# Even mixer of an encoder trunk: rotary partner added by transfers, load phase by arrival, residual kept in DRAM

## The chip, the cores and the metric

The kernel runs on one core of a Trainium2 chip. The metric is the device time of one execution in microseconds (us), lower is better. The core has TensorE (PE, with its weight loads PEld), VectorE (DVE), ScalarE (ACT), GpSimd (POOL) and SyncE (SP), which here only issues transfers. Each engine works through its own instructions in order and waits at semaphores for the others.

## What is computed

The reference is an encoder trunk of two layers with 512 positions of 1024 channels in float32. Cut to what matters:

```
for i in 0, 1:
    h += 0.5 * SwiGLU_1(RMSNorm(h))            # 1024 -> 2 x 2816 -> 1024
    if i == 0:   h += W_out [A | B]            # the even mixer
    else:        h += W_out NA2D(RMSNorm(h))   # the odd mixer
    h += 0.5 * SwiGLU_2(RMSNorm(h))
    h += sigmoid(RMSNorm(h) @ W_gate) * (p[i] @ W_ple)
out = RMSNorm(h)

A: 12 query heads and 4 key/value heads of 64, window |i-j| <= 128,
   a sink logit per head, rotary positions on q and k
B: 4 slots, each with three dilated windows (128,1), (512,4), (2048,16),
   rotary, the three outputs merged by their softmax denominators
```

The rotary step takes a projection p of two heads (128 channels x 512 positions) to p*cos + partner(p)*sin, where the partner of a channel lies 32 channels away in the same head.

## The kernel before

Activations lie with channels on the 128 partitions and the 512 positions along the row, eight chunks of 128 channels for h. Every float32 product is made of three matmuls on parts: a value is split into a high part, rounded to the matmul's type, and a low part, the rest; `mm3` (L154) multiplies high by high, high by low and low by high. Weights come in units of 128x1024 (512 KB) by SP's queue into `wr`; `split` (L132) makes the high part on ScalarE (L133, a copy) and the low part by a subtraction (L134) on VectorE, or in the mixers for every third unit on GpSimd (`lo_eng`, L136). The pool of activations has 62 tiles of 128x512, the small pool `tmp` ten. PSUM has three banks `mm`, two `sc`, two `tr` and one `ob`.

**The load phase.** `setup` (L96) runs idle matmuls first (WARM, L112). It loads the eight chunks of h, the gate unit after chunk 0 and the up unit after chunk 5 (UP_AT), and writes the splits of the chunks (`norm_split`, L183 on ScalarE and L184 on VectorE) and of the units as code in chunk order; a scheduler sets the final order by priorities. `pair_front` (L235) then multiplies all of the gate unit and all of the up unit, 24 matmuls each.

**Feed-forwards.** Four pairs go through `pair_front`, a pair at 4 through `pair`, and the pairs from 5 on through `pair_fast` (L298), which multiplies with fewer products on sums of halves. One of its sums of weights is made by an accumulating transfer on GpSimd's queue (L308), and its half unit `rb` is a tile of the small pool (L304). The residual is stored to DRAM when a feed-forward begins and loaded again in its down projection (L369 to L391). In the even mixer h stays in SBUF.

**The even mixer.** `ab` (L584) builds two lists. The steps are softmax and value steps: `a_steps` (L679) with scores and softmax of a head (`a_soft`, L706; scores at L575, mask, scaling and maximum at L576) and the product with the values (transposes at L496, products at L507), and `b_steps` (L722) with scores, softmax and a merge over the three windows (L758 on; its scalings at L785, its transposes at L794). The fill is TensorE work that needs no softmax: 20 projections of 24 matmuls, four value projections of 96 shorter ones and parts of the output projection. `weave` (L650) puts fill between the steps by weights and by what each step needs; then `out_proj` (L530) does the rest and adds h.

The norm's factor R comes from sums of squares by `stat` (L199): matmuls, a scaling on VectorE (L206), a power on GpSimd (L207), a transposition on TensorE (L223). `rope` (L541) multiplies R into the tables of cosines and sines once. Then, for every projection, VectorE shuffles lanes within groups of 32 (L551) and multiplies by the cosines (L552), GpSimd multiplies the shuffled copy by the sines (L553), and VectorE adds both (L556, L559, L562, by the order in which positions are written). For this, weights lie in memory with the channels of a head permuted, so that a partner is 16 lanes away. `stack_q` (L409) puts the high and low part of a query, 64 lanes each, above each other (L416 on ScalarE, L417 on VectorE). `stack_k` (L421) does the like for keys with a copy by SP's queue (L429), a subtraction on GpSimd (L430) into tiles whose other half is zeroed (L439). The finished mixture is split with its low part on GpSimd (`split_chunk`, L674).

## Time and profile before

| | us |
|---|---|
| median of three runs | 2096.43 |
| the three runs | 2096.35, 2096.43, 2098.21 |
| the profiled execution | 2097.75 |
| its span on the core | 2095.8 |

The profiled execution's time includes 1.95 us outside the span. Its granted TensorE clock has a mean of 0.993. The page has busy times by engine; rows of the view by windows give the same for one stretch, with the number of instructions in brackets. A row of the waits names the engine and line that waited, the engine, tile and line that ended the wait, and the us in total, the times and the longest. A row of the timeline has start and duration, in brackets the idle time before it and what ended that. Rows by groups have the count, then busy us and mean ns, then idle time before; rows by line have the least, median and greatest duration in ns. Line numbers in rows of before are those of the code above.

| stretch, us of the span | stage |
|---|---|
| 0 to 26 | load phase and first pair |
| 26 to 367 | rest of the first feed-forward |
| 367 to 652 | even mixer, with its output projection |
| 652 to 1030 | second feed-forward |
| 1030 to 2096 | gated embedding, layer 1, last norm |

### The profile page before, as it was taken

The page shows a single profiled execution, that of the slowest core. Times are in us where ns is not written, and L with a number is a line of the kernel's source. Part 1 is how long each engine was busy: PE and PEld are TensorE (multiplying, and loading weights), DVE is VectorE, ACT ScalarE, POOL GpSimd, SP SyncE. Part 2 cuts the span into 40 slices and gives each one's busy share as a digit, 9 for nine tenths or more (in the row PEclk, how much of TensorE's full clock was granted, in tenths as well). Part 3 has the DMA queues.
Part 4 walks back from the last instruction along what each step waited for, and adds up shares of the span by engine and source line. Part 5 has one row for each costly group of instructions (what it writes and reads, how often), then busy time and mean ns, then how long its engine had stood idle before and what let it go on. Part 6 is the DMA issues. An engine that isn't in the chain of part 4 may idle for free.

```text
span 2095.8 us, 31959 instructions
## 1 busy us (share of the span) xinstructions
PE 2047.1 (98%) x12400; PEld 1813.2 (87%) x12400; DVE 1403.4 (67%) x2449; ACT 978.1 (47%) x1661; POOL 284.1 (14%) x221
## 2 busy tenths in 40 slices
PE   9999999999999999999999999999999999999998
PEld 6999988777787899988888999888888789998886
DVE  7878733699786887752459877434778787775334
ACT  5455522565544455442345555323656545554232
POOL 0000011233211000001110000013222200000111
PEclk9999999999999999999999999999999999999999
DMA  6666533221223466643334665433333346665331
GB/s 181 164 178 173 161 119 109 92 70 56 66 68 130 111 170 165 169 151 114 118 129 122 176 167 158 146 119 121 106 106 97 120 110 169 171 169 151 108 113 41
DMA packets 103063, 270.59 MB, mean 129 GB/s; under 512 B 19968, under 2 KB 27648, under 8 KB 102912
## 3 DMA queue, kind: packets, MB, share of 16 engines
q1 hardware_dynamic: 92976, 232.87, 34.2%
q0 software_dynamic: 9792, 35.66, 10.2%
q8 instruction: 97, 1.59, 0.3%
q14 instruction: 54, 0.44, 0.1%
q10 hardware_dynamic: 144, 0.04, 0.0%
HBM read 253.83 MB, written 8.88 MB: 125 GB/s over the span
## 4 chain that ended last, share of the span: by engine, by line
PE 82%; DVE 7%; ACT 4%; DMA 4%; issue 2%; POOL 1%; SPq 0%; ACTq 0%; DVEq 0%; POOLq 0%
PE mm L158 9%; PE mm L159 9%; PE mm L157 9%; PE sc L157 6%; PE sc L159 6%; PE sc L158 6%; PE mm L330 5%; PE mm L331 5%; PE mm L332 5%; DMA tmp<-in_gu_dram 3%; PE sc L332 2%; PE sc L331 2%; PE sc L330 2%; DVE wl L134 2%; ACT wh L133 2%
## 5 line engine op out<-in xcount | busy, mean ns | idle before, releaser
L133 ACT ACTIVATE wh<-wr 128x1024 fp32r<-128x1024 f32 (+2 forms) x430 | 439.2, 1035 | 669.3 <-PE mm L158 180.8
L134 DVE TENSOR_TENSOR wl<-wr,wh 128x1024 fp32r<-128x1024 f32 (+2 forms) x413 | 501.0, 1217 | 319.7 <-ACT wh L133 317.8
L157 PE MATMUL mm<-act,wh 128*128 128x512 f32 (+1 forms) x1016 | 399.0, 393 | 2.8 <-ACT act L183 2.4
L158 PE MATMUL mm<-act,wh 128*128 128x512 f32 (+1 forms) x1016 | 400.0, 394 | 1.4 <-POOL act L134 0.6
L159 PE MATMUL mm<-act,wl 128*128 128x512 f32 (+1 forms) x1016 | 398.1, 392 | 0.0
L330 PE MATMUL mm<-act,wh 128*128 128x256 f32 x1088 | 312.9, 288 | 7.6 <-ACT tmp L348 4.2
L332 PE MATMUL mm<-act,wl 128*128 128x256 f32 x1088 | 308.2, 283 | 0.0
L331 PE MATMUL mm<-act,wh 128*128 128x256 f32 x1088 | 308.2, 283 | 0.0
L159 PE MATMUL sc<-act,wl 128*128 128x512 f32 (+1 forms) x594 | 231.4, 389 | 0.6 <-DVE wl L134 0.6
L157 PE MATMUL sc<-act,wh 128*128 128x512 f32 (+1 forms) x594 | 231.9, 390 | 0.0
L158 PE MATMUL sc<-act,wh 128*128 128x512 f32 (+1 forms) x594 | 231.4, 390 | 0.0
L157 PEld LDWEIGHTS mm<-act,wh 128*128 128x128 f32 x1016 | 191.8, 189 | 41.2 <-ACT act L183 3.6
L158 PEld LDWEIGHTS mm<-act,wh 128*128 128x128 f32 x1016 | 192.1, 189 | 40.5 <-DVE act L184 2.4
L159 PEld LDWEIGHTS mm<-act,wl 128*128 128x128 f32 x1016 | 192.1, 189 | 36.4
L330 PEld LDWEIGHTS mm<-act,wh 128*128 128x128 f32 x1088 | 208.5, 192 | 14.3 <-ACT tmp L348 8.4
L331 PEld LDWEIGHTS mm<-act,wh 128*128 128x128 f32 x1088 | 208.7, 192 | 0.3
L332 PEld LDWEIGHTS mm<-act,wl 128*128 128x128 f32 x1088 | 208.7, 192 | 0.2
L197 POOL TENSOR_TENSOR ssq<-ssq,tmp 128x512 f32<-128x512 f32 x48 | 78.4, 1634 | 684.6 <-ACT tmp L190 684.5
L332 PE MATMUL sc<-act,wl 128*128 128x256 f32 x544 | 155.1, 285 | 1.5 <-DVE wl L134 1.5
L330 PE MATMUL sc<-act,wh 128*128 128x256 f32 x544 | 154.7, 284 | 1.0 <-ACT wh L133 0.8
L331 PE MATMUL sc<-act,wh 128*128 128x256 f32 x544 | 154.1, 283 | 0.0
L308 POOL DMA_DIRECT2D wr<-in_gu_dram x68 | 59.2, 871 | 699.4 <-DMA wr<-in_gu_dram 244.9
(180 smaller groups left out, 3541.9 us busy)
## 6 DMA issues: line engine op xcount, KB each, us to landing
wr<-in_gu_dram SPq DMA_DIRECT2D x176, 512.0 KB, 4.1
wr<-in_gu_dram POOLq DMA_DIRECT2D x68, 512.0 KB, 5.4
wr<-in_dn_dram SPq DMA_DIRECT2D x64, 512.0 KB, 3.8
tmp<-in_gu_dram SPq DMA_DIRECT2D x68, 256.0 KB, 4.6
wr<-in_dn_dram SPq DMA_DIRECT2D x32, 384.0 KB, 3.2
wr<-in_qk_ab_dram SPq DMA_DIRECT2D x20, 512.0 KB, 3.2
wr<-in_plg_dram SPq DMA_DIRECT2D x16, 512.0 KB, 3.2
wr<-in_qk_c_dram SPq DMA_DIRECT2D x16, 512.0 KB, 3.3
```

Of the source, the lines that this page charges most:

```text
L133: self.nc.scalar.activation(hi, src, AF.Copy)
L134: (lo_eng or self.nc.vector).tensor_tensor(lo, src, hi.bitcast(F32), op=ALU.subtract)
L157: mm(out, stat[0], mov[0], start=start, stop=False)
L158: mm(out, stat[0], mov[1], start=False, stop=False)
L159: mm(out, stat[1], mov[0], start=False, stop=stop)
L197: eng.tensor_tensor(self.acc, self.acc, sq, op=ALU.add)
L308: nc.gpsimd.dma_start(rs, w[:, :UNIT], accum_op=ALU.add)
L330: mm(out, w[0][:, c], xs[k][0][:, x], start=start and k == 0, stop=False, skip_group_check=True)
L331: mm(out, w[0][:, c], xs[k][1][:, x], start=False, stop=False, skip_group_check=True)
L332: mm(out, w[1][:, c], xs[k][0][:, x], start=False, stop=stop and k == half - 1, skip_group_check=True)
```

## The change

It has six parts.

1. **Load phase.** WARM goes from 14 to 12 and UP_AT from 5 to 3. The splits of chunks and units are written six chunks behind the loads (LEAD), in the order in which the data are to arrive, with the gate unit in three pieces, and the scheduler keeps that order. The first pair's up products start at k = 3 between the gate products. The next pair's units come behind the last split.
2. **Rotary partner by transfers.** The lanes are no longer permuted. VectorE multiplies the projection by the sines into `u` and by the cosines into `o` (after L595, L596), already in the order wanted; four accumulating transfers of 32x512 (64 KB) on GpSimd's queue then add `u` to `o`, each 32 lanes to the 32 beside them (after L599). The mixer has 20 such steps, so 80 transfers.
3. **Stacks a chunk later.** `stacked` parts the projection and rotary step from the stack, and `behind_next` puts each stack behind the next fill item.
4. **No arithmetic on GpSimd in the even mixer**, but for the power and the zeroing: low parts of weights, of keys and of the mixture go to VectorE, and the two wide scalings of each A softmax (L719) to ScalarE. The mixture's split comes a step later (`split_later`).
5. **Start and weave.** The first two projections go to the two `sc` banks ahead of the norm's factor; six fill items come ahead of the first softmax step; A steps weigh 1.3 for 1; two B steps claim what they need two steps earlier (BEGIN_B).
6. **Tiles.** The even mixer stores h to DRAM and loads it in its output projection (`put_away`, `fetch`). The small pool has eight tiles instead of ten, and `rb` two of its own.

The diff, cut to this:

```diff
-WARM = 14
+WARM = 12
-UP_AT = 5
+UP_AT = 3
+LEAD = 6
-TMPS = 10
+TMPS = 8
+BEGIN_B = 26, 32
...
+        pieces = {0: ((0, 0, q), (0, q, 2 * q)), 1: ((0, 2 * q, UNIT),), UP_AT: ((1, 2 * q, UNIT), (1, 0, 2 * q))}
+        self.pinned = True
+        for n in range(KC + LEAD):
...
+            c = n - LEAD
+            if c >= 0:
+                last = self.norm_split(c)
+                for j, a, b in pieces.get(c, ()):
+                    self.split(*(y[:, a:b] for y in units[j]))
...
-        return self.nc.vector if self.turn else self.nc.gpsimd
+        return self.nc.vector if self.turn or self.alone else self.nc.gpsimd
...
+                for k in range(KC):
+                    self.mm_pair(pgu[0], gate, self.xg, 0, (k,))
+                    if k >= UP_AT:
+                        self.mm_pair(pgu[1], u, self.xg, 1, (k - UP_AT,))
+                self.mm_pair(pgu[1], u, self.xg, 1, range(KC - UP_AT, KC))
...
-        rb = self.tmp()
+        rb = self.tp.tile([P, T], F32, tag="rb", name=self.nm("rb"), bufs=2)
...
-            nc.gpsimd.tensor_tensor(low[hf][own, :], k[own, :], t[own, :].bitcast(F32), op=ALU.subtract)
+            eng = nc.vector if self.alone else nc.gpsimd
+            eng.tensor_tensor(low[hf][own, :], k[own, :], t[own, :].bitcast(F32), op=ALU.subtract)
...
-            nc.vector.stream_shuffle(t2, p, mask=[(i + 16) % 32 for i in range(32)])
-            nc.vector.tensor_tensor(t1, p, self.cosr, op=ALU.mult)
-        nc.gpsimd.tensor_tensor(t2, t2, self.sinr, op=ALU.mult)
...
+            nc.vector.tensor_tensor(v(u), w(p), w(self.sinr), op=ALU.mult)
+            nc.vector.tensor_tensor(v(o), w(p), w(self.cosr), op=ALU.mult)
+        for i in range(4):
+            j = i ^ 1
+            nc.gpsimd.dma_start(o[i * 32:(i + 1) * 32, :], u[j * 32:(j + 1) * 32, :], accum_op=ALU.add)
...
+        p = [self.project(w[12 + i], self.sbank()) for i in range(2)]
+        with self.tc.issue_after(self.last_mm.ins):
+            self.R
+        fill = behind_next(stacked(("ak", 0), 12, "n", p[0]), stacked(("aq", 0, 0), 13, "n", p[1]), proj_v("va", 0),
+                           *proj_a(0)[2:], *proj_a(1), *proj_b(0), proj_v("vb", 1), proj_v(("vr", 0), 2),
+                           *proj_b(1), proj_v(("vr", 1), 3))
...
+        for _ in range(6):
+            fill.pop(0)[2]()
+        kept = self.put_away()
...
+        for i in BEGIN_B:
+            steps[i - 2] = steps[i - 2][0] + steps[i][0], *steps[i - 2][1:]
...
-            nc.vector.tensor_scalar_mul(es[b], es[b], rd[:, b:b + 1])
+            r = rd[:, b:b + 1]
+            if 0 < b < NB - 1:
+                nc.scalar.activation(es[b], es[b], AF.Copy, scale=r)
+            else:
+                nc.vector.tensor_scalar_mul(es[b], es[b], r)
```

What moves on an engine shows in its order of instructions: the line, the operation, the tile written and those read with their numbers, and the shape. First ScalarE in the load phase, before. `wh_119` and `wh_133` are the high parts of the gate and the up unit, the L183 rows the high parts of h's chunks.

```order
L133 ACTIVATE wh_119<-wr_118 128x256
L133 ACTIVATE wh_119<-wr_118 128x768
L183 ACTIVATE act_140<-act_116,gain 128x512
L183 ACTIVATE act_148<-act_122,gain 128x512
L133 ACTIVATE wh_133<-wr_132 128x256
L183 ACTIVATE act_152<-act_124,gain 128x512
L133 ACTIVATE wh_133<-wr_132 128x768
L183 ACTIVATE act_156<-act_126,gain 128x512
```

And the same place after the change, where `wh_117` is the gate unit's, `wh_127` the up unit's high part and L197 what L183 was.

```order
L197 ACTIVATE act_136<-act_114,gain 128x512
L147 ACTIVATE wh_117<-wr_116 128x256 x2
L197 ACTIVATE act_146<-act_120,gain 128x512
L147 ACTIVATE wh_117<-wr_116 128x512
L197 ACTIVATE act_152<-act_122,gain 128x512
L197 ACTIVATE act_156<-act_124,gain 128x512
L147 ACTIVATE wh_127<-wr_126 128x512 x2
L197 ACTIVATE act_164<-act_130,gain 128x512
```

The first four chunks (`act_136` to `act_156`) now come ahead of the up unit, and the gate unit's second half stands behind chunk 1; before, the whole gate unit stood ahead of any chunk and the up unit's first piece ahead of the third.

Next GpSimd at the start of the even mixer, before: weight splits (L134), the power (L207), products with the sines (L553), zeroing (L439) and the keys' low parts (L430).

```order
L134 TENSOR_TENSOR wl_3688<-wr_3686,wh_3687 128x1024
L134 TENSOR_TENSOR wl_3922<-wr_3920,wh_3921 128x1024
L207 TENSOR_TENSOR rcol_3656<-ms_3655,mhalf 128x4
L553 TENSOR_TENSOR tmp_3668<-tmp_3668,act_3648 128x512
L439 MEMSET act_3674 64x512
L439 MEMSET act_3676 64x512
L553 TENSOR_TENSOR tmp_3718<-tmp_3718,act_3648 128x512
L430 TENSOR_TENSOR act_3674<-act_3672,act_3678 64x512
L430 TENSOR_TENSOR act_3676<-act_3672,act_3682 64x512
```

The same place after the change; the L599 rows are the partner's transfers, four to a row.

```order
L222 TENSOR_TENSOR rcol_3685<-ms_3684,mhalf 128x4
L474 MEMSET act_3714 64x512
L599 DMA act_3698<-tmp_3699 32x512 x4
L599 DMA act_3706<-tmp_3707 32x512 x4
L474 MEMSET act_3716 64x512
L599 DMA act_3885<-tmp_3886 32x512 x4
L599 DMA act_4001<-tmp_4002 32x512 x4
```

The power has nothing of the mixer ahead of it any more, and the queue holds transfers and zeroing where it held arithmetic.

Last VectorE around the first rotary steps, before: shuffle and cosines (L551, L552), the sum (L556), a weight split (L134), the first query's stack (L417) and the first score's mask (L576, printed as ISA).

```order
L552 TENSOR_TENSOR tmp_3667<-mm_3622,act_3647 128x512
L556 TENSOR_TENSOR act_3672<-tmp_3667,tmp_3668 128x512
L551 STREAM_SHUFFLE tmp_3718<-mm_3692 128x512
L552 TENSOR_TENSOR tmp_3717<-mm_3692,act_3647 128x512
L134 TENSOR_TENSOR wl_4123<-wr_4121,wh_4122 128x1024
L556 TENSOR_TENSOR act_3722<-tmp_3717,tmp_3718 128x512
L417 TENSOR_TENSOR act_3724<-act_3722,act_3724 64x512
L417 TENSOR_TENSOR act_3727<-act_3722,act_3727 64x512
L576 ISA act_3732,st_a_3730<-sc_3731,act_3608 128x256
```

After the change, with L465 the key's low parts and L519 the low parts of the values.

```order
L595 TENSOR_TENSOR tmp_3699<-sc_3616,act_3695 128x512
L595 TENSOR_TENSOR tmp_3707<-sc_3647,act_3695 128x512
L596 TENSOR_TENSOR act_3698<-sc_3616,act_3694 128x512
L596 TENSOR_TENSOR act_3706<-sc_3647,act_3694 128x512
L148 TENSOR_TENSOR wl_4060<-wr_4058,wh_4059 128x1024
L148 TENSOR_TENSOR wl_4181<-wr_4179,wh_4180 128x1024
L465 TENSOR_TENSOR act_3714<-act_3698,act_3718 64x512
L519 SCALAR_TENSOR_TENSOR act_3836<-mm_3726,rcol_3685,act_3836 128x4x64
L465 TENSOR_TENSOR act_3716<-act_3698,act_3722 64x512
```

Both rotary steps now stand side by side, two weight splits stand between them and the key's low parts, and the evictions of the values stand behind these.

More of the change, by code (lines that the diff above doesn't have):

```diff
@@ L65, in __init__ @@
         self.ahead = []
+        self.pinned = self.alone = False
+        self.later = []
         self.open = {}
@@ L158, in mm3 @@
         mm(out, stat[0], mov[1], start=False, stop=False)
-        mm(out, stat[1], mov[0], start=False, stop=stop)
+        return mm(out, stat[1], mov[0], start=False, stop=stop)
     def mm_unit(self, out, u, xs, start, stop):
@@ L164, in mm_unit @@
             w = (u[0][:, i * P:(i + 1) * P], u[1][:, i * P:(i + 1) * P])
-            self.mm3(out, w, x, start and i == 0, stop and i == len(xs) - 1)
+            self.last_mm = self.mm3(out, w, x, start and i == 0, stop and i == len(xs) - 1)
     def begin_norm(self, k):
@@ L246, in pair_front @@
         if m == 0 and first:
+            with ExitStack() as s:
+                for ins in self.last:
+                    s.enter_context(self.tc.issue_after(ins.ins))
+                self.ahead = [self.unit(ahead[:, (1 - j) * UNIT:(2 - j) * UNIT]) for j in range(2)]
             for c in range(KC):
@@ L388, in ffn @@
         for m in range(KC):
-            for c in range(m + 1 if m else 0, min(m + 2, KC)):
-                self.h[c] = self.act()
-                nc.sync.dma_start(self.h[c], kept[c])
+            self.fetch(kept, m)
             p = self.sbank() if m % 2 else self.bank()
@@ L399, in ffn, with put_away, fetch, project @@
             self.norm_chunk(m)
-    def project(self, src):
+    def put_away(self):
+        kept = self.dp.tile([KC, P, T], F32, name=self.nm("kept"))
+        for c in range(KC):
+            self.nc.sync.dma_start(kept[c], self.h[c])
+        return kept
+    def fetch(self, kept, m):
+        for c in range(m + 1 if m else 0, min(m + 2, KC)):
+            self.h[c] = self.act()
+            self.nc.sync.dma_start(self.h[c], kept[c])
+    def project(self, src, p=None):
         u = self.unit(src, lo_eng=self.lo_eng())
-        p = self.bank()
+        p = p or self.bank()
         self.mm_unit(p, u, self.xg, True, True)
@@ L645, in ab, with behind @@
         fill += [(("o", m), PART, lambda m=m: self.out_part(io["o_ab"], m, mix, range(6))) for m in range(OPEN)]
-        self.weave(steps, fill, after={("o", 0): 26})
-        self.out_proj(io["o_ab"], mix, 6, k_next)
+        for _ in range(6):
+            fill.pop(0)[2]()
+        kept = self.put_away()
+        first = steps[0][2]
+        def behind():
+            with self.tc.issue_after(self.last_mm.ins):
+                first()
+        steps[0] = steps[0][0], steps[0][1], behind
+        for i in BEGIN_B:
+            steps[i - 2] = steps[i - 2][0] + steps[i][0], *steps[i - 2][1:]
+        self.weave(steps, fill, after={("o", 0): BEGIN_B[0]})
+        self.alone = False
+        self.out_proj(io["o_ab"], mix, 6, k_next, kept)
     @staticmethod
@@ L677, in split_chunk, with split_later @@
         return hi, lo
+    def split_later(self, mix):
+        for c, raw in self.later:
+            mix[c] = self.split_chunk(raw, self.nc.vector)
+        self.later = []
     def a_steps(self, gp, t, v, m_a, sink, mix):
@@ L1121, in _constants @@
     cos = np.cos(ang).astype(f32).T[j]
-    sin = np.sin(ang).astype(f32).T[j] * np.where(first, -1, 1).astype(f32)[:, None]
+    sin = np.sin(ang).astype(f32).T[j] * np.where(first, 1, -1).astype(f32)[:, None]
     add = lambda ok: np.where(ok, 0.0, NEG).astype(f32)
```

142 lines of the change are left out of this document (69 added, 73 removed).

## The prediction

> **What bounds the kernel now.** The page comes first. Its first lines give the busy time of each engine and, after x, its instructions.
>
> ```profile
> span 2095.8 us, 31959 instructions
> PE 2047.1 (98%) x12400; PEld 1813.2 (87%) x12400; DVE 1403.4 (67%) x2449; ACT 978.1 (47%) x1661; POOL 284.1 (14%) x221
> ```
>
> TensorE is busy for 98% of the span, so the change, which leaves its products as they are, can win only what TensorE loses to waits and to a low granted clock. The view by windows says where that is: each row has the window, its length, the busy time of PE, PEld, DVE, ACT and POOL, the granted clock, the DMA share and GB/s. I cut the span at the load phase, the front pairs, the first feed-forward, the even mixer and, after it, the second feed-forward.
>
> ```profile
> 0.00:26.00 26.00, 21.71 (x64) 13.63 (x65) 16.65 (x25) 16.29 (x26) 0.20 (x4) 0.80 0.77 269
> 70.00:372.00 302.00, 300.03 (x1979) 276.07 (x1978) 185.71 (x247) 131.16 (x197) 25.12 (x21) 1.00 0.54 153
> 372.00:652.00 280.00, 261.25 (x1518) 218.98 (x1517) 224.01 (x591) 145.02 (x345) 72.64 (x51) 0.98 0.19 63
> 652.00:1030.00 378.00, 375.48 (x2321) 338.71 (x2320) 246.63 (x333) 169.69 (x251) 37.48 (x30) 1.00 0.52 148
> ```
>
> The feed-forwards lose 2 to 3 us each. Two stretches lose more: the load phase (26.00 - 21.71 = 4.3 us idle, and a mean clock of 0.80) and the even mixer (280.00 - 261.25 = 18.75 us idle, and 0.98). The change touches just these two. In the mixer VectorE is busy for 224.01/280 = 80%. Next, the waits of TensorE in the mixer: what waited, for what, us in all, times, longest.
>
> ```profile
> PE tr L496 <- DVE act L719: 5.0, 5, 1.6
> PE tr L794 <- DVE act L785: 4.3, 2, 2.6
> PE ob L507 <- DVE tmp L134: 2.6, 3, 1.4
> PE sc L575 <- DVE act L417: 2.5, 1, 2.5
> PE tr L223 <- POOL rcol L207: 1.5, 1, 1.5
> ```
>
> These five make 15.9 us of the 18.75. Four of them end on VectorE. The low clock stands in two windows of the mixer, by the same view:
>
> ```profile
> 541.30:548.00 6.70, 6.23 (x25) 5.70 (x25) 3.62 (x13) 6.13 (x21) 0.00 (x0) 0.50 0.01 2
> 561.80:565.00 3.20, 2.82 (x8) 2.34 (x9) 3.20 (x8) 0.00 (x0) 1.61 (x2) 0.50 0.16 51
> ```
>
> At half clock, 6.23 + 2.82 = 9.05 us of work would have taken 4.5 us: 4.5 us lost. The profiled execution took 2097.75 us, 1.3 us above the median of 2096.43; I sum against it and take off 1.3 at the end. A run can tell about 0.2% (4.2 us) from no change.
>
> **Load phase.** The same view at the half-clock windows and behind them, and two matmuls of the timeline (start, duration):
>
> ```profile
> 8.80:12.10 3.30, 2.50 (x5) 1.49 (x5) 1.21 (x3) 0.74 (x2) 0.00 (x0) 0.50 1.06 410
> 12.20:15.50 3.30, 3.06 (x6) 1.70 (x7) 3.11 (x6) 3.30 (x6) 0.00 (x0) 0.50 1.03 397
> 15.60:18.90 3.30, 3.30 (x10) 2.53 (x9) 3.30 (x4) 3.30 (x6) 0.00 (x0) 0.50 1.02 411
> 19.10:25.50 6.40, 6.40 (x29) 5.26 (x29) 5.88 (x9) 4.21 (x8) 0.00 (x0) 1.00 0.43 115
> 8.07 0.49 PE L157 MATMUL mm<-act,wh 128*128 128x512 f32 x1 [1.57 <-ACT act L183]
> 25.55 0.39 PE L157 MATMUL mm<-act,wh 128*128 128x512 f32 x1
> ```
>
> The first pair's 48 matmuls run from 8.07 to 25.55. TensorE idles in the first two windows, and full clock comes only after the first window in which it doesn't. At full clock 29 take 6.6 us, 0.227 each; at half clock a step takes twice that less a little, 0.427. The window 15.60:18.90 holds some 8 steps, so only 48 - 29 - 8 = 11 are done by 15.6. The changed order gives ScalarE and VectorE the splits in the order of arrival, so chunks 0 to 3 (12 matmuls) no longer stand behind the gate unit's 768 columns, and products of the up unit fill in from k = 3 on. If the first window fills, the clock opens at 12.2 with some 10 done, and 38 x 0.227 = 8.6 ends at 20.8: -4.7. If the second is the first full one, it opens at 15.5 with 18 done: 15.5 + 30 x 0.227 = 22.3: -3.2. With gaps left in both and 13 done: 23.5, -2. I take **-3.5**, range -5 to -2.
>
> The Trainium skill, "TensorE: Matmul & The Clock Gate", Part 1, says that full clock is released by one busy window of a free-running counter (about 3.4 us), so the gain would come in such steps, and -4.7 or -3.2 rather than a value between. The rows above agree, three windows of 3.3 us.
>
> **Start of the mixer.** The mixer's first matmul on TensorE, GpSimd's queue, and TensorE's first score with two value matmuls behind it:
>
> ```profile
> 367.43 0.39 PE L157 MATMUL mm<-act,wh 128*128 128x512 f32 x1
> 374.03 2.39 POOL L134 TENSOR_TENSOR wl<-wr,wh 128x1024 fp32r<-128x1024 f32 x1 [12.56 <-ACT wh L133]
> 376.38 1.04 POOL L207 TENSOR_TENSOR rcol<-ms,mhalf 128x4 f32<-128x4 f32 x1
> 388.79 0.85 PE L575 MATMUL sc<-act,act 128*128 128x256 f32 x4 [2.54 <-DVE act L417]
> 389.48 0.28 PE L469 MATMUL mm<-wh,act 128*128 128x256 f32 x1
> 389.60 0.28 PE L470 MATMUL mm<-wl,act 128*128 128x256 f32 x1
> ```
>
> The power behind the norm stands behind a 2.39 us split on GpSimd; that split goes to VectorE, and the 1.5 us wait ends. The first score waits 2.5 us for a stack. In the new order two projections (48 matmuls of 0.227), the A values (96 of 0.12, by the two rows) and 35 more matmuls stand ahead of it, so that 19.4 us of TensorE's work lie between the two projections and the score: the wait ends as well. **-4.0**. Nothing is late next there, as these matmuls read the normed chunks and weights alone, which are there.
>
> **VectorE and GpSimd.** One timeline row of GpSimd with one of VectorE, the groups of the operations concerned (count, then busy and mean ns), and the transfers' rows (KB each, us to landing):
>
> ```profile
> 431.04 2.36 POOL L134 TENSOR_TENSOR wl<-wr,wh 128x1024 fp32r<-128x1024 f32 x1 [10.13 <-ACT wh L133]
> 431.48 2.99 DVE L719 TENSOR_SCALAR act<-act,st_a 128x256 f32<-128x256 f32 x4
> L719 DVE TENSOR_SCALAR act<-act,st_a x48: 340/408/2484, 396.8 to 529.8; 128x256 f32<-128x256 f32 x24, 128x384 f32<-128x384 f32 x24
> L134 DVE TENSOR_TENSOR wl<-wr,wh 128x1024 fp32r<-128x1024 f32 x21 | 27.9, 1331 | 0.7 <-ACT wh L133 0.7
> L719 DVE TENSOR_SCALAR act<-act,st_a 128x256 f32<-128x256 f32 x24 | 16.5, 690 | 0.2
> L551 DVE STREAM_SHUFFLE tmp<-mm 128x512 f32<-128x512 f32 x20 | 15.0, 749 | 0.0
> L552 DVE TENSOR_TENSOR tmp<-mm,act 128x512 f32<-128x512 f32 x20 | 13.5, 675 | 0.1
> L417 DVE TENSOR_TENSOR act<-act,act 64x512 fp32r<-64x512 f32 x16 | 12.9, 805 | 1.1 <-ACT act L416 0.7
> L719 DVE TENSOR_SCALAR act<-act,st_a 128x384 f32<-128x384 f32 x24 | 9.4, 417 | 0.0
> L559 DVE TENSOR_TENSOR act<-tmp,tmp 128x512 f32<-128x512 f32 x8 | 8.8, 1095 | 0.5 <-POOL tmp L553 0.4
> L556 DVE TENSOR_TENSOR act<-tmp,tmp 128x512 f32<-128x512 f32 x10 | 7.9, 793 | 0.8 <-POOL tmp L553 0.8
> L134 POOL TENSOR_TENSOR wl<-wr,wh 128x1024 fp32r<-128x1024 f32 x8 | 19.7, 2466 | 55.5 <-ACT wh L133 41.2 <-issue 10.4 <-PE mm L159 4.0
> L308 POOL DMA_DIRECT2D wr<-in_gu_dram x14: 862/862/865, 77.7 to 215.1; - x14
> wr<-in_gu_dram POOLq DMA_DIRECT2D x68, 512.0 KB, 5.4
> act<-act SPq DMA_DIRECT2D x8, 128.0 KB, 2.2
> ```
>
> VectorE loses the shuffles (15.0) and the adds (8.8 + 7.9 + 2 more of about 1.1 = 18.9). It gains 20 products, 20 x 0.675 = 13.5 (up to 6 more where they write in the order that made L559 0.3 us dearer than L556), 8 weight splits (8 x 1.331 = 10.6), 8 lows (8 x 0.805 = 6.4) and 6 mixture splits of half a unit's size (6 x 0.67 = 4.0); ScalarE takes the 24 wide scalings (9.4). Net: 13.5 + 10.6 + 6.4 + 4.0 - 15.0 - 18.9 - 9.4 = -8.8 us, at worst -2.8. ScalarE, 145.02 of 280, has room for 24 more. Then the hold: the 128x256 scaling that starts at 431.48 is the longest, 2484 ns against a least of 340, and lies across the GpSimd split that ends at 433.40. Its group has a mean of 690: 24 x 0.35 = 8.4 us of stretching in this one group. It is what L496 waits for. With no arithmetic on GpSimd I take off **-5.5** of the 5.0 + 2.6 us of L496 and L507 (range -7.6 to -2).
>
> The first B merge (L794, 4.3 us) waits for VectorE with 29 value matmuls and 25 others ahead of it as cover (29 x 0.12 + 25 x 0.227 = 9.2 us); in the new order 61 of the longer kind (13.8 us) stand there. The second merge keeps its 28. I take **-2.6** (the longer of the two waits), range -4.3 to -1.3. The two half-clock windows follow such gaps: **-3** of 4.5, range -4.5 to 0.
>
> **What it adds.** 80 accumulating transfers of 64 KB on GpSimd's queue: 80 x 0.862 = 69 us of issuing where 72.64 us were busy. No row has one from SBUF: the landing lies between 2.2 us (128 KB, SBUF to SBUF, SP's queue) and 5.4 us (512 KB, accumulated, GpSimd's queue). I take 2.2, as it has the nearest size and source. Two products 1.35, four issues 3.45, landing 2.2, stack 2 x 0.8 = 1.6: 8.6 us from projection to stack, against a chunk's slot of 280/28 = 10 us, since the stack comes a chunk later. It fits, with little to spare. VectorE's queue has the stack's subtractions in order, and value evictions and softmax steps behind them, for which TensorE waits. For 12 stacks I put **+3**, a quarter us each; range 0 to the third rival's price. The memsets stay. The residual's 8 stores and 8 loads of 256 KB go through SP's queue at a DMA share of 0.19, ahead of no unit that is due within 2 us: 0. The half-unit tile gets its own two buffers and the small pool gives up two: 0 in the feed-forwards, which lose 2 us in 302, range -3 to +3.
>
> Sum: -3.5 - 4.0 - 5.5 - 2.6 - 3 + 3 = -15.6. 2097.75 - 15.6 = 2082.1; less 1.3: **2081**.
>
> **Rivals.** (1) The hold stays: GpSimd's 69 us of issuing stop VectorE as its 72.64 us of arithmetic did. For it: as much time. Against it: 14 issues in the first feed-forward took 862 to 865 ns beside a VectorE busy for 61%, with no sign that either waited. The -5.5 goes: 2081 + 5.5 = 2086.5. Chance 0.15.
> (2) The softmax chain starts late: 48 + 35 matmuls of 0.227 and 96 of 0.12 are 30.4 us; from 367.43 on that puts the first score at 397.8, 9.0 us behind its place of 388.79, and the fills used there are missing at the end, where the steps then wait on each other. The start's -4.0 gives nothing, and 9 us come back: -15.6 + 4.0 + 9.0 = -2.6, so 2093.8. For it: VectorE at 80%. Against it: before the first merge more fill stands than before. Chance 0.12.
> (3) The partner comes late, and the kernel is slower. With a landing of 6.3 us, a microsecond above the accumulating row's, the way from projection to stack is 12.7 us, 2.7 over the slot; in 12 stacks 32 us. Less the gains of 18.6: +13.8, so 2110. It decides from a landing of about 5.2 us on, where 12 x 1.55 us eat up the 18.6. For it: four issues must pass one after the other, and VectorE is busy meanwhile. Against it: the constant 862 ns. Chance 0.11.
>
> The Trainium skill, "SBUF — State Buffer", "SBUF: two separate sides", warns of rival 3: descriptors of a GpSimd-issued DMA wait while VectorE holds the shared port, with 3100 ns for a transfer of 620 ns. By that, an estimate, four transfers could be 4 x 2.5 = 10 us later. The row of 862 ns doesn't show it; whether it does so for SBUF sources no run here shows.
>
> **How the numbers follow.** The forecast has 0.62 and its own range, from its bounds, of 2066 to 2094. Rival 1 lies inside it, rival 2 at its upper end. A range of 2067 to 2096 leaves out rival 3 and small tails. Faster than 2092.2: most of the forecast (0.59), of rival 1 (0.14) and a third of rival 2 (0.04): 0.77. Between 2092.2 and 2100.6: 0.13. Slower: rival 3, 0.10.
>
> **What would show it.** Right: the second pair starts at 21 to 23.5; L719's longest is under 0.8 us; the power runs at once; no half clock in the mixer; TensorE idles under 8 us in the mixer. Wrong: waits of TensorE or VectorE on the accumulating transfers of 10 us or more, landings above 5 us, or scores that wait at the end of the mixer without fill.

## The result, and the profile after

The changed kernel takes 2059.04 us (median of four runs, 2057.28 to 2061.43) against 2096.39 us beside it: 1.8% less, the ratio 0.9823 with a 95% interval of 0.9806 to 0.9840. The forecast was 2081 with a range of 2067 to 2096. The gain is 37.4 us instead of 15: the sign was right, the size too small by more than half. The profiled execution took 2057.28 us. The head of its page:

```profile
span 2055.5 us, 32176 instructions
PE 2024.6 (98%) x12398; PEld 1803.9 (88%) x12398; DVE 1389.8 (68%) x2409; ACT 1002.2 (49%) x1686; POOL 278.1 (14%) x258
```

TensorE is still busy for 98% of the span: by that share alone nothing has happened. Where the 40.3 us between the two spans went is read from marks that both traces have: the first start of the fast pairs' line (L330 before, L358 after), the last start of it in each feed-forward, the last addition of a down projection (L398, L419) and of the output projection (L537, L574).

The mixer's stage includes all of its output projection and so ends later, at 676.6 before, than the 652 at which the forecast cut it.

| stage | before, us | after, us | difference | forecast |
|---|---|---|---|---|
| start to the first fast pair | 55.6 | 50.7 | -4.9 | -3.5 |
| fast pairs, first feed-forward | 191.8 | 186.8 | -5.0 | 0 |
| fast pairs, the other three | 550.5 | 532.6 | -17.9 | 0 |
| even mixer | 309.0 | 295.9 | -13.1 | -12.1 |
| all else | 988.9 | 989.5 | +0.6 | 0 |

More than half of the gain, 22.9 us, lies in the fast pairs, where the change had only given the half-unit tile `rb` a place of its own and taken two tiles from the small pool. The row by windows for the second feed-forward's fast pairs, of before:

```profile
725.90:909.00 183.10, 180.58 (x1454) 177.07 (x1453) 146.04 (x207) 97.25 (x155) 12.04 (x14) 1.00 0.61 166
```

And of after, over the same work:

```profile
702.90:880.40 177.50, 177.50 (x1455) 176.28 (x1453) 146.89 (x208) 100.43 (x155) 12.22 (x14) 1.00 0.64 172
```

The stage is 5.6 us shorter, yet TensorE's idle time fell only by 183.10 - 180.58 = 2.5 us; the other 3.1 us had been inside its busy time. The rows of the line that waited show how. Of before, with the least, median and greatest duration in ns:

```profile
L330 PE MATMUL mm<-act,wh x1088: 274/283/388, 55.6 to 1906.4; 128*128 128x256 f32 x182
```

Of after:

```profile
L358 PE MATMUL mm<-act,wh x1088: 277/283/284, 50.7 to 1865.5; 128*128 128x256 f32 x182
```

A matmul here is shown for 283 ns, while the next starts 120 ns later. A start that is late by up to 0.16 us is covered by the tail of the one before and never appears as idle, and some rows are longer. So the 2 us of idle time in 302 by which the forecast put the feed-forwards at nothing was a lower bound of the loss.

What they waited for stands in ScalarE's waits. Before, in the same stretch (what waited, for what, us in all, times, longest):

```profile
ACT wh L133 <- DVE wr L320: 35.9, 15, 3.0
ACT tmp L356 <- DVE tmp L355: 24.9, 16, 2.3
ACT wh L133 <- DMA tmp<-in_gu_dram: 12.6, 14, 2.0
...
ACT tmp L348 <- PE mm L332: 1.1, 3, 0.5
```

After:

```profile
ACT wh L147 <- DVE wr L348: 18.3, 10, 2.1
ACT tmp L384 <- DVE tmp L383: 17.6, 15, 1.4
...
ACT tmp L376 <- PE mm L360: 7.2, 16, 0.5
```

Before, ScalarE waited in 14 of 17 pairs for `rb` to land, and its copy of a product out of PSUM (L348), which stands behind that split in its queue, came late for TensorE: only in 3 pairs was ScalarE there first. After, it waits for TensorE in 16 of 17, and not for the transfer. SP's queue shows why the load was late. Of before, start and duration of each issue:

```profile
750.94 0.33 SPq L309 DMA_DIRECT2D wr<-in_gu_dram  x1
751.32 0.49 SPq L306 DMA_DIRECT2D tmp<-in_gu_dram  x1
754.31 0.33 SPq L307 DMA_DIRECT2D wr<-in_gu_dram  x1
```

And its use on ScalarE:

```profile
757.44 0.63 ACT L133 ACTIVATE wh<-tmp 128x512 fp32r<-128x512 f32 x1 [0.50 <-DMA tmp<-in_gu_dram]
```

Of after, issue by issue:

```profile
724.58 0.33 SPq L334 DMA_DIRECT2D rb<-in_gu_dram  x1
727.78 0.33 SPq L337 DMA_DIRECT2D wr<-in_gu_dram  x1
731.14 0.33 SPq L335 DMA_DIRECT2D wr<-in_gu_dram  x1
```

Before, the 256 KB of `rb` were issued 0.4 us behind a 512 KB load of the next pair (L309) and 6.1 us ahead of their use, and it took them just these 6.1 us to land. The load at L309 had waited for VectorE, as it does 14 times in this stretch by SP's waits:

```profile
SPq L309 <- DVE tmp L351: 104.4, 14, 9.1
```

After, `rb` goes 3.2 us ahead of that load. This holds for nearly all pairs: before, 15 of the 17 loads of `rb` stand 0.4 us behind a load of L309; after, 14 of 17 stand 3.2 to 4.1 us ahead of one. The median from issue to landing is 4.5 us before and 2.7 us after.

The page of before had said it. Its part on the chain that ended last, by line:

```profile
PE mm L158 9%; PE mm L159 9%; PE mm L157 9%; PE sc L157 6%; PE sc L159 6%; PE sc L158 6%; PE mm L330 5%; PE mm L331 5%; PE mm L332 5%; DMA tmp<-in_gu_dram 3%; PE sc L332 2%; PE sc L331 2%; PE sc L330 2%; DVE wl L134 2%; ACT wh L133 2%
```

"DMA tmp<-in_gu_dram 3%" are some 60 us of the chain on the transfers of one tile. The forecast quoted no line of this part.

In the mixer, TensorE's waits after the change:

```profile
PE tr L870 <- DVE act L861: 5.7, 2, 3.8
PE tr L238 <- POOL rcol L222: 1.8, 1, 1.8
PE ob L542 <- DVE tmp L148: 0.8, 1, 0.8
PE sc L612 <- DVE st_b L613: 0.5, 1, 0.5
PE sc L612 <- DVE st_a L613: 0.4, 2, 0.3
```

The waits on the A scaling and on the parts of the transposes (7.6 us before) are down to 0.8, the first scores' 2.5 are gone. The merges' wait has grown from 4.3 to 5.7, and that on GpSimd's power is 1.8 instead of 1.5. The half clock is down from 10.2 us to one window behind the first merge:

```profile
557.30:560.70 3.40, 3.40 (x12) 2.54 (x11) 3.40 (x12) 0.45 (x1) 0.00 (x0) 0.50 0.00 0
```

In the load phase the clock of this execution never fell:

```profile
0.00:26.00 26.00, 22.00 (x88) 14.77 (x89) 18.05 (x28) 17.20 (x27) 0.92 (x5) 1.00 0.85 305
```

### The profile page after: what moved, and what is told of

Read it like the earlier page. It is cut to its first block, busy times and chain, and to the rows that moved or that the text cites. A ratio compares the mean times of both kernels' runs of the same rounds, so it can differ in the third digit from the quotient of the medians.

```text
span 2055.5 us, 32176 instructions
## 1 busy us (share of the span) xinstructions
PE 2024.6 (98%) x12398; PEld 1803.9 (88%) x12398; DVE 1389.8 (68%) x2409; ACT 1002.2 (49%) x1686; POOL 278.1 (14%) x258
## 4 chain that ended last, share of the span: by engine, by line
PE 87%; DVE 6%; ACT 2%; issue 2%; DMA 1%; POOL 1%; SPq 0%; DVEq 0%; ACTq 0%; POOLq 0%
PE mm L172 9%; PE mm L173 9%; PE mm L171 9%; PE mm L360 6%; PE mm L358 6%; PE mm L359 6%; PE sc L171 6%; PE sc L173 6%; PE sc L172 6%; PE sc L358 3%; PE sc L360 3%; PE sc L359 3%; PE ob L359 2%; PE ob L360 2%; PE ob L358 2%
## 5 line engine op out<-in xcount | busy, mean ns | idle before, releaser
L147 ACT ACTIVATE wh<-wr 128x1024 fp32r<-128x1024 f32 (+2 forms) x431 | 446.2, 1037 | 647.3 <-PE mm L172 180.4
L148 DVE TENSOR_TENSOR wl<-wr,wh 128x1024 fp32r<-128x1024 f32 (+2 forms) x423 | 511.4, 1211 | 326.4 <-ACT wh L147 324.1
L171 PE MATMUL mm<-act,wh 128*128 128x512 f32 (+1 forms) x1000 | 391.6, 392 | 1.6 <-ACT wh L147 0.9
L172 PE MATMUL mm<-act,wh 128*128 128x512 f32 (+1 forms) x1000 | 391.2, 391 | 1.5 <-POOL act L148 0.6
L173 PE MATMUL mm<-act,wl 128*128 128x512 f32 (+1 forms) x1000 | 390.6, 391 | 0.0
L358 PE MATMUL mm<-act,wh 128*128 128x256 f32 x1088 | 308.0, 283 | 0.0
L173 PE MATMUL sc<-act,wl 128*128 128x512 f32 x610 | 237.3, 389 | 0.4 <-DVE wl L148 0.4
L171 PE MATMUL sc<-act,wh 128*128 128x512 f32 x610 | 237.5, 389 | 0.0
L172 PE MATMUL sc<-act,wh 128*128 128x512 f32 x610 | 237.4, 389 | 0.0
L358 PEld LDWEIGHTS mm<-act,wh 128*128 128x128 f32 x1088 | 208.9, 192 | 0.2
L358 PE MATMUL sc<-act,wh 128*128 128x256 f32 x544 | 154.0, 283 | 0.0
```

The lines of the kernel that those rows point to most:

```text
L147: self.put(self.nc.scalar.activation(hi, src, AF.Copy))
L148: self.put((lo_eng or self.nc.vector).tensor_tensor(lo, src, hi.bitcast(F32), op=ALU.subtract))
L171: mm(out, stat[0], mov[0], start=start, stop=False)
L172: mm(out, stat[0], mov[1], start=False, stop=False)
L173: return mm(out, stat[1], mov[0], start=False, stop=stop)
L358: mm(out, w[0][:, c], xs[k][0][:, x], start=start and k == 0, stop=False, skip_group_check=True)
```

## The experiments

For the feed-forwards there were two theories. A: the late load of `rb` held ScalarE and by it TensorE. B: the fast pairs gained through something else in the change. For the mixer, C: GpSimd's arithmetic held VectorE; D: the gain is the new order. The kernel before had medians of 2092.3 to 2096.9 us beside the various runs, so that times of two runs that had different runs of it beside them compare to about 4 us; the lengths of the stages in the traces are finer.

| run | us | ratio to before, 95% | fast pairs, us | mixer, us |
|---|---|---|---|---|
| before | 2096.39 | 1 | 742.3 | 309.0 |
| changed | 2059.04 | 0.9806 to 0.9840 | 719.4 | 295.9 |
| e1_rb_own | 2074.27 | 0.9886 to 0.9938 | 719.5 | 310.3 |
| e2_rb_back | 2081.15 | 0.9925 to 0.9957 | 744.0 | 297.2 |
| e3_load_old | 2063.64 | 0.9841 to 0.9890 | 719.5 | 298.6 |
| e4_rb_one | 2058.37 | 0.9816 to 0.9868 | 719.4 | 300.1 |
| e5_rb_actq | 2077.33 | 0.9911 to 0.9936 | 719.8 | 310.2 |
| m1_gpsimd_back | 2077.47 | 0.9915 to 0.9943 | 719.4 | 316.1 |
| m2_no_later | 2080.08 | 0.9928 to 0.9957 | 719.4 | 324.1 |
| m3_double_issues | 2063.19 | 0.9847 to 0.9874 | 719.4 | 301.8 |
| n1_rope_back | 2058.10 | 0.9805 to 0.9848 | 719.3 | 298.3 |
| n2_lows_back | 2071.08 | 0.9868 to 0.9905 | 719.3 | 310.0 |
| n3_start_old | 2059.16 | 0.9810 to 0.9854 | 719.4 | 297.9 |
| n4_early_merge | 2058.98 | 0.9809 to 0.9851 | 719.3 | 297.2 |
| q1_rope_no_later | 2064.42 | 0.9848 to 0.9877 | 719.4 | 303.0 |
| q2_rcol_early | 2055.27 | 0.9805 to 0.9833 | 719.4 | 294.2 |
| q3_lows_in_before | 2078.25 | 0.9914 to 0.9944 | 719.5 | 311.4 |

The stages are those of the one profiled execution of each run. A window of 3.4 us at half clock in the mixer moves its length by about 1.7 us. The changed kernel and q2_rcol_early had one such window there, the others two to four, m1_gpsimd_back six and m2_no_later nine; by that, an estimate, 8.5 of the 20 us by which m1's stage is longer and 14 of m2's 28 are half clock.

**e1_rb_own.** The kernel before, one part of the change alone:

```diff
-TMPS = 10
+TMPS = 8
-        rb = self.tmp()
+        rb = self.tp.tile([P, T], F32, tag="rb", name=self.nm("rb"), bufs=2)
```

> The kernel before with one part of the change alone: rb in two tiles of its own, the small pool with eight tiles. Theory A (rb's late load held ScalarE, and by it TensorE, in the fast pairs): 23 us faster than before, 2073 us, and ScalarE's waits on the rb transfer gone. Theory B (the fast pairs gain through the rest of the change, and rb's place is nothing): within 4 us of before.

It took 2074.27 us, 19.3 us less than the 2093.54 beside it, and its fast pairs took 719.5 us: as long as the changed kernel's to 0.1 us. ScalarE's waits in the second feed-forward's fast pairs no longer have the transfer, and read like those of the changed kernel:

```profile
ACT wh L133 <- DVE wr L320: 18.3, 10, 2.1
ACT tmp L356 <- DVE tmp L355: 17.5, 15, 1.4
ACT wh L133 <- ACT wh L133: 10.2, 16, 1.0
ACT tmp L348 <- PE mm L332: 7.2, 16, 0.5
```

**e2_rb_back.** The changed kernel with the converse edit (`TMPS = 10`, `rb = self.tmp()`).

> The changed kernel with rb back in the small pool, which has ten tiles again. Theory A: 23 us slower than the changed kernel, 2082 us. Theory B: within 4 us of the changed kernel's 2059.

2081.15 us, 22.1 more than the changed kernel; fast pairs 744.0. The wait is back:

```profile
ACT wh L147 <- DVE wr L348: 34.2, 15, 3.0
ACT tmp L384 <- DVE tmp L383: 24.9, 16, 2.3
ACT wh L147 <- DMA tmp<-in_gu_dram: 12.8, 11, 1.9
```

In SP's queue 15 of the 17 loads of `rb` stand 0.4 to 0.7 us behind one of L337 again; with e1_rb_own 14 of 17 stand 3.2 to 4.1 us ahead of it, as in the changed kernel. The edit costs about the same both ways, 22.8 and 24.6 us by the stage, 19.3 and 22.1 by the times: theory A, and B falls.

**e4_rb_one.** The changed kernel with `bufs=1` for `rb`.

> The changed kernel with one tile for rb instead of two. Under theory A the gain comes from an earlier load; with one tile the load can start only when the pair before has split its rb, one pair (10.1 us) ahead of its use, and still 2.7 us of transfer fit: no change, 2059 us. If the second tile is what gives the gain: 10 to 23 us slower.

2058.37 us, fast pairs 719.4: no change. One tile is enough: the gain is not that of a second buffer.

**e5_rb_actq.** The kernel before, `rb` in the pool of ten, on another queue:

```diff
-        dma(rb, w[:, :M])
+        nc.scalar.dma_start(rb, w[:, :M])
```

> The kernel before, rb still in the small pool of ten tiles, but its transfer issued on ScalarE's queue instead of SP's, so that it no longer stands behind the load of a later pair there. If the place in SP's queue made it late: 15 to 20 us faster than before, about 2077. If the release of the small pool's tile did: no change, 2093 to 2096, as the transfer waits for its tile on any queue.

2077.33 us, 15.0 less than the 2092.33 beside it, and fast pairs of 719.8 us. With the tile's pool unchanged, leaving SP's queue gives the whole 22.5 us of the stage. (By the times it is 15.0; the kernel before has only one trace, whose execution took 2097.75 us, where its runs beside these here have a median of 2092.33.) On its own queue the load of `rb` is issued up to 1.8 us ahead of one of L309 in 14 of 17 pairs. So the cause is the place behind another load that waits for its buffer, and the own tile helped by letting the scheduler set the load elsewhere in the queue. The landing is 3.4 us at the median in the second feed-forward, and waits for it remain (9.4 us in 6 pairs, by the rows of the line), but not where TensorE feels them.

**e3_load_old.** The changed kernel with `setup` and the first pair's order of before, and with WARM 14 and UP_AT 5.

> The changed kernel with the load phase and the first pair of before (WARM 14, UP_AT 5, splits in the scheduler's order, gate products ahead of up products). If the load phase gave what the two traces differ by at the first fast pair: 4.9 us slower than the changed kernel, 2064 us. If the clock's fall in the first windows is an accident of the execution: no difference.

2063.64 us, 4.6 more, as expected. In its profiled execution the first fast pair starts at 54.1 us instead of 50.7, and 6.8 us run at half clock from 9.2 on. The load phase gives 3.4 us by the stage and 4.6 by the times.

**m1_gpsimd_back.** All of GpSimd's arithmetic of before, in the new order: the `rope` of before (as in the diff above, with the lanes permuted) and

```diff
-        self.turn, self.alone = 1, True
+        self.turn, self.alone = 1, False
-            mix[c] = self.split_chunk(raw, self.nc.vector)
+            mix[c] = self.split_chunk(raw)
```

> The changed kernel with the arithmetic on GpSimd in the even mixer as before: shuffle, product with the sines on GpSimd and a sum on VectorE in the rotary step (weights' lanes permuted again), every third low part of a weight, the keys' and the mixture's low parts on GpSimd. The order (start, stacks a chunk later, weights of the steps), the scalings on ScalarE, the residual in DRAM and the load phase stay. Theory C (GpSimd's arithmetic held VectorE): 6 to 8 us slower than the changed kernel, about 2066, with waits on the A scaling and on the parts of the transposes back. Theory D (the mixer's gain is the new order): within 3 us of 2059.

2077.47 us, 18.4 more; the mixer takes 316.1 us, 7 more than before the change. So D falls as it was put: the new order without the moved arithmetic is slower than the old one. C had the sign, and less than half of the size. The waits that it named come back in part, the A scaling with 1.7 us and the parts of the transposes with 3.5, but those on the merges grow to 8.9 and those of the scores to 6.4 as well.

**n1_rope_back.** Of these two, the rotary step alone as before; low parts stay on VectorE.

> The changed kernel with the rotary step of before alone: shuffle and sum on VectorE, product with the sines on GpSimd, weights' lanes permuted; the low parts stay on VectorE. Theory C1 (both kinds of GpSimd arithmetic hold VectorE, in proportion to their 25.8 and 41.6 us): about 7 of the 18 us that both cost together, 2066. Theory C2 (the rotary step alone carries it, since VectorE now has the low parts as well and the sum waits for GpSimd in VectorE's queue): 13 us or more slower than the changed kernel, 2072 or more.

2058.10 us: no change. Both C1 and C2 said it would be slower.

**n2_lows_back.** The low parts alone back on GpSimd (the diff shown with m1_gpsimd_back), the partner by transfers.

> The changed kernel with the low parts of every third weight, of the keys and of the mixture back on GpSimd; the rotary partner stays with the transfers. Theory C1: about 11 us slower, 2070. Theory C2: at most 5 us slower, 2064.

2071.08 us, 12.0 more, close to C1's 2070. But the two parts don't add in proportion: 0 and 12, and 18 together. The hold shows in VectorE's 128x256 scaling, least, median and greatest duration in ns. With the low parts on GpSimd:

```profile
L794 DVE TENSOR_SCALAR act<-act,st_a x24: 334/354/1747, 402.2 to 526.7; 128x256 f32<-128x256 f32 x24
```

With the rotary product alone on GpSimd:

```profile
L794 DVE TENSOR_SCALAR act<-act,st_a x24: 336/350/1115, 402.3 to 525.0; 128x256 f32<-128x256 f32 x24
```

In the changed kernel:

```profile
L794 DVE TENSOR_SCALAR act<-act,st_a x24: 334/350/452, 399.3 to 516.0; 128x256 f32<-128x256 f32 x24
```

The rotary product takes 1.29 us on average, about half of what a unit's split takes, 2.47. In the traces of before, n1_rope_back and m1_gpsimd_back all 11 of these scalings that took over 600 ns end 0.15 us behind a GpSimd instruction that had begun ahead of them; in n2_lows_back four of six do. So a held scaling mostly waits out what is left of the GpSimd instruction under way, which is less for the product than for the split. TensorE's longest wait in n2_lows_back is not on this scaling, though, but on the merges:

```profile
PE tr L870 <- DVE act L861: 10.4, 2, 8.6
PE ob L541 <- ACT tmp L147: 3.8, 2, 3.0
PE sc L612 <- DVE st_a L613: 2.6, 3, 1.2
```

**m2_no_later.** The changed kernel with the stacks at once:

```diff
         def behind_next(*items):
 
-            out, rest = [], []
-            for first, *second in items:
-                out += [first] + rest
-                rest = second
-            return out + rest
+            return [x for item in items for x in item]
```

> The changed kernel with each stack right behind its rotary step instead of a fill item later. Theory C: the partner's landing, about 8 us behind the projection, now stands in front of the scores: 5 us or more slower in the few places where a stack is due at once, 2064. If the landing is covered anyway: no change, 2059.

2080.08 us, 21.0 more, and the mixer 28 us longer in its profiled execution, with 20.4 us of half clock in the stage's first 140 us. Theory C had the sign and a quarter of the size. It is the dearest part to undo. ScalarE's waits say what the later stack covers:

```profile
ACT act L450 <- DMA act<-tmp: 12.4, 9, 4.0
...
ACT act L462 <- DMA act<-tmp: 9.1, 4, 4.4
```

ScalarE stands 21.5 us in front of stacks (L450 queries, L462 keys) whose partner has not landed, with weight splits, transposes and softmax steps behind them in its order. In the changed kernel the same wait is 0.2 us.

**q1_rope_no_later.** The same edit on n1_rope_back, so without transfers.

> The changed kernel with the rotary step of before and each stack right behind its rotary step; low parts on VectorE, start and the rest as changed. Theory L1 (the later stack pays for the transfers' landing alone): without transfers nothing to cover, 2058 as with the rotary step of before alone. Theory L2 (the later stack pays by itself, as work behind a stack waits in VectorE's and ScalarE's order whatever makes the partner): 10 to 20 us slower, 2068 to 2078.

2064.42 us, 6.3 more than n1_rope_back. The time lies between the two theories: a later stack is worth 6 us by itself, and the other 15 are the landing that it covers. So without later stacks the transfers cost 15.7 (2080.08 against 2064.42), and with them they are level with the rotary step of before.

**m3_double_issues.** Twice the issues for the same bytes:

```diff
-            nc.gpsimd.dma_start(o[i * 32:(i + 1) * 32, :], u[j * 32:(j + 1) * 32, :], accum_op=ALU.add)
+            for x in (slice(0, T // 2), slice(T // 2, T)):
+                nc.gpsimd.dma_start(o[i * 32:(i + 1) * 32, x], u[j * 32:(j + 1) * 32, x], accum_op=ALU.add)
```

> The changed kernel with the partner added by 8 transfers of 32x256 instead of 4 of 32x512: 160 issues where there were 80, for the same result. If issuing and landing are hidden with room (no wait on them in the trace of the changed kernel over 1 us): at most 3 us slower, 2059 to 2062. If they fill their slot, as the third rival had it: each rotary step 5 us later and 20 us or more slower, 2080.

2063.19 us, 4.2 more: a little over what hidden transfers were to cost, hardly more than such times can be told apart, and far from 20. The slot has room, but not for twice as much: the mixer is 5.9 us longer, stacks wait 6.8 us for landings by the rows of the line, and the median landing is 3.9 us.

**n3_start_old.** The changed kernel without its start: no projections ahead of the factor, no six items ahead of the first softmax step.

> The changed kernel with the mixer's start as before: no projections ahead of the norm's factor, no six fill items ahead of the first softmax step, which isn't tied to a matmul. Stacks a chunk later, transfers and low parts stay. If the start gives what I forecast for it: 4 us slower, 2063, with a wait of 2 us or more at the first scores. If the cover of the first ropes matters as much as the later stacks do: 10 us slower or more, 2069.

2059.16 us: the start is worth nothing, where both expectations had a loss. The first scores, at 388.6, don't wait: up to 420 TensorE's only wait in this trace's mixer is that on the power, 1.8 us. What covers them without the start, the later stacks perhaps, was not tried.

**n4_early_merge.** Two edits for the waits that are left:

```diff
-        p = [self.project(w[12 + i], self.sbank()) for i in range(2)]
+        p = [self.project(w[12], self.sbank())]
+        with self.tc.issue_after(self.last_mm.ins):
+            self.rcol
+        p.append(self.project(w[13], self.sbank()))
...
+        def early():
+            with self.tc.high_priority():
+                merge()
```

> The changed kernel with two waits shortened that its trace still shows: the norm's column factor is asked for behind the first of the two projections instead of behind both (its power on GpSimd, 1.8 us of waiting), and the two merges' operations get priority in VectorE's order (5.7 us of waiting, and the half clock behind the first). If those waits end: 2052 to 2056. If VectorE's other work, now behind the merges, is late instead: 2059.

2058.98 us. The wait on the power is gone, but the merges wait longer, 7.5 us where it was 5.7:

```profile
PE tr L877 <- DVE act L864: 7.5, 2, 5.1
PE sc L612 <- DVE st_a L613: 0.5, 2, 0.3
```

That is the second expectation's time, without its cause. In the trace the priority has not taken the other work out: between 547.2 and 552.2, inside the first merge, VectorE still has a rotary step's two products, three subtractions for stacks and a low part of the mixture (L595, L596, L465, L451, L148), and the merge's own 32 small copies take 6 us. Whether that work makes the merge late stays untested.

**q2_rcol_early.** The first of these edits alone.

> The changed kernel with one edit: the norm's column factor asked for behind the first of the two projections. The wait of 1.8 us on GpSimd's power ends, the merges stay as they are: 2057, 1 to 2 us faster than the changed kernel; if the time moves into the first scores' wait, 2059.

2055.27 us (2054.65 to 2056.41), ratio 0.9805 to 0.9833: 3.8 us less than the changed kernel's median. The mixer of its trace is 1.7 us shorter, which is the 1.8 us wait; the rest is within the 4 us. It is the fastest version here.

**q3_lows_in_before.** The kernel before with `rb`'s own tiles and the low parts on VectorE, rotary step, stacks, start and order as before.

> The kernel before with rb's own tiles and, in the even mixer, the low parts of weights, keys and mixture on VectorE; rotary step, stacks, start and order as before. Theory M1 (the low parts' move is worth its 12 us in any order): the mixer falls from 310 to about 298 us, 2062 in all. Theory M2 (it needs the later stacks): the mixer stays within 4 us of 310, 2072 to 2076.

2078.25 us, the mixer 311.4: no gain over e1_rb_own, if anything a loss of some us. M2 had the mixer right, within 4 us of 310, and its time, 2072 to 2076, a little low: moving the low parts is worth 12 us in the new order and nothing in the old one. That it is the later stacks which the low parts need, as M2 had it, is not shown: no run has these two alone.

## Why the prediction was wrong

**The feed-forwards: the step that failed.** The term was 0 with bounds of -3 and +3, from an idle time of 2 us in 302. It measured -22.9 us by the stages, 19 to 22 by the times of e1_rb_own and e2_rb_back, and these two show that this one edit carries all of it. The change of SP's order could have been read from the order of the two programs, as it was for ScalarE, GpSimd and VectorE, and the price from the profile of before: 12.6 us of waiting by ScalarE for that tile in one feed-forward, and 3% of the last chain. The step took TensorE's idle time for its loss, where up to 0.16 us per start hides in the busy time, and looked at the tile's pool rather than at what stands ahead of its transfer. Put right, the sum would have been -15.6 - 22.9 = -38.5, and the time 2058; that this is within a microsecond of the measured time is partly luck, as the terms below miss in both directions.

**Load phase.** -3.5 forecast, -4.9 measured at the first fast pair, 4.6 when undone. The first part of the mechanism, splits in the order of arrival, was right and was worth more: the second pair starts at 19.5 instead of 25.55, earlier than the 21 to 23.5 that were named as the sign, and the second pair, which the forecast left out, gives 1.1 us back. The second part, the clock, decided less. With the old order half clock lasted 10.2 us (before), 6.8 (q3_lows_in_before and e3_load_old) or 3.4 (e1_rb_own), and the first fast pair started at 55.6, at 55.1 and 54.1, or at 54.7. With the new one it lasted 3.4 us in e4_rb_one, behind the first pair, and none in the changed kernel, and the first fast pair started at 52.2 and 50.7. So with one such window in both, the new order is still 2.5 us ahead. Half clock came in whole windows of 3.4 us, as the Trainium skill, "TensorE: Matmul & The Clock Gate", Part 1, has it; the gain did not come in such steps, and no counted case had a load phase without half clock.

**Start of the mixer.** -4.0 forecast; the 2.5 us of the first scores went, the 1.5 us of the power became 1.8. The power has nothing ahead of it on GpSimd now, as forecast, but it starts only at 369.6:

```profile
369.61 2.01 POOL L222 TENSOR_TENSOR rcol<-ms,mhalf 128x4 f32<-128x4 f32 x1 [22.92 <-DVE ms L221]
```

The matmuls of the norm's sums stand behind both projections in TensorE's order, which the forecast had not looked up; q2_rcol_early puts them between the two, and the wait ends. The power also takes 2.01 us instead of 1.04 (see the last section). The 2.5 us are no gain of the start: without it they are gone too (n3_start_old).

**VectorE's hold.** -5.5 of 7.6 forecast; the waits fell by 6.8. The mechanism stands: the greatest duration of the scaling fell from 2484 to 452 ns, and rises with GpSimd's arithmetic. The forecast took the scaling at 431.48 for the longest; that one took 2067 ns, and the one of 2484 ns starts at 480.21, across another split. VectorE's busy time in the stage fell from 245.7 to 228.1 us, by 17.7, which is close to the -8.8 of moved work and the 8.4 of stretching together. But it is the low parts that count, and only in the new order.

**Merges and half clock.** -2.6 forecast, +1.4 measured; the 61 matmuls of cover are there where 54 were, but the wait ends later. VectorE's queue now has a weight split, stacks and a rotary product between the merge's operations; that these make it late is argued, not shown. Half clock: -3 forecast, -3.4 measured (10.2 us down to 3.4, at half the work).

**New waits.** +3 forecast; TensorE has none over 1 us. GpSimd's issues and the transfers' landing, with the range in ns and then in us:

```profile
L599 POOL DMA_DIRECT2D act<-tmp x80: 775/1382/2907, 376.8 to 579.0; - x80
...
DMA to landing us min/median/max: 2.4/3.2/6.6
```

The median of 1382 ns is not what an issue costs. Four issues start 0.50 us apart and end 0.80 us apart, so that their durations overlap and grow, 775, 1080, 1385 and 1690 ns, and the 2907 is the last of eight in a row. A step's four take 3.18 us in all, where 3.45 was forecast:

```profile
408.24 3.18 POOL L599 DMA_DIRECT2D act<-tmp  x4 [5.92 <-issue]
```

The Trainium skill, "SBUF — State Buffer", "SBUF: two separate sides", says that GpSimd can't write the descriptors of such transfers while VectorE holds the port that both share. This trace doesn't show it: one after the other, the issues end 0.80 to 0.89 us apart, whatever VectorE does meanwhile. With a later stack the transfers cost nothing, without one 15 us.

**The mixer's sum.** -12.1 was forecast for the stage and -13.1 measured, which is luck in part: the merges missed by +4.0 and the start by +1.8 or more, and the +3 for new waits didn't come. TensorE's idle time in the stage fell from 18.75 to 10.4 us, not to under 8 as named for a sign.

**The rivals.** Rival 1 (the hold stays by the issues) is out: the scaling isn't stretched. Rival 2's late start came true, the first scores being 33.6 us behind the stage's start instead of 21.2, 12.4 us later, without its cost. Rival 3's mechanism is real and is what m2_no_later measures; the later stacks are what keeps it away.

**What stays open.** The mixer's 13 us are not a sum of parts. The rotary partner by transfers, the largest part of the change, brings nothing that shows: with the rotary step of before the kernel is as fast. Undone one at a time, four parts cost 0 (rotary transfers), 0 (start), 12 (low parts) and 21 (later stacks); the low parts alone in the old order bring nothing, and the new order with GpSimd's arithmetic loses 7. Why they need one another is argued, not shown: the new order has VectorE and ScalarE work further ahead and is more easily held. The scalings on ScalarE, the weights of the steps, the earlier needs of the B steps and the residual in DRAM were not tried by themselves.

## What to carry to other kernels

Read the chain's share by line to its end, and price every transfer in it: a tile at 3% of the chain is worth more than the share of idle time lets one expect, since closely pipelined matmuls hide small delays in their busy time. When a tile moves to another pool, look at what its transfer then stands behind in the queue that issues it, and where it will stand after. When a step gets a longer latency, such as a partner by transfer, undo each of them in an experiment before crediting either: here the transfers alone cost 15 us, the later stacks hid that, and the kernel with the later stacks and without the transfers is as fast as with both.

## What the runs showed of the hardware

A GpSimd power on 128x4 (L222) took 1.02 to 1.04 us at four of its eight places in the changed kernel and 1.94 to 2.01 at the other four. At these four, the mixer's among them, VectorE had begun a weight split (L148, 1.2 us) up to 0.16 us ahead of it. At one of them the split began 0.19 us behind the power in m3_double_issues, and the power took 1.02 us.

VectorE's product of a PSUM bank with a table (L595) took 680 to 694 ns for the ten projections in plain order, and 1060 to 1129 ns for the ten that write their rows in a rearranged order; the row has the 18 of them that read a bank `mm`:

```profile
L595 DVE TENSOR_TENSOR tmp<-mm,act x18: 680/1061/1129, 389.3 to 574.8; 128x512 f32<-128x512 f32 x18
```
